# Eleven pad tiles in the SBUF pools of a one-core diffusion block: another start address for the operands of its matmuls

## The chip, the cores and the metric

The kernel runs on one core of one Trainium2 chip. It uses TensorE (PE in the profile, with PEld for its loads of the stationary operand), VectorE (DVE), ScalarE (ACT), GpSimd (POOL) and SyncE (SP), which issues all loads from HBM. The metric is the device time of one execution in microseconds (us); lower is better. SBUF, the core's working memory, has 128 partitions, and a tile lies at the same byte address in each of them. "Phase" below means the start address of an operand in its partition, modulo 256 bytes. "Distance" means the phase of a matmul's moving operand less the phase of its stationary operand, again modulo 256.

## The reference

One block works on 256 latent tokens (`x`) with 256 context tokens (`ctx`), 1024 channels, one layer, all in float32. Cut to what sets the work:

```python
mod = silu(c) @ w_ada + b_ada                       # 9 vectors, for x and for ctx
x   = x   + 0.5 * g1 * swiglu(modulate(rmsnorm(x)),   w13_ffn1, w2_ffn1)   # d_ff 2816
ctx = ctx + 0.5 * g1 * swiglu(modulate(rmsnorm(ctx)), w13_ffn1, w2_ffn1)
q, k, v, g, f, ga, gf = split(modulate(rmsnorm(.)) @ w_in)   # ctx: k and v alone are needed
o   = bidirectional retention, 4 heads (dk 256, dv 512), state from ctx, then x
r   = (silu(g) * groupnorm(o)) @ p_ret
fo  = real(fft2(f over tokens and 256 channels of a group)) @ p_four
x   = x + g2 * ((sigmoid(ga) * r + sigmoid(gf) * fo) @ w_out)
x   = x + 0.5 * g3 * swiglu(modulate(rmsnorm(x)), w13_ffn2, w2_ffn2)
return rmsnorm(x)
```

## The kernel before

Channels lie on partitions and tokens on the free axis. Every float32 product is made of three fp32r matmuls: a weight tile is loaded as `wr`, rounded by ACT into `wh` (line 78), and DVE (sometimes POOL) writes the remainder `wl` (line 79). The activations are split into a high and a low tile in the same way (`split`, lines 82 to 84). `mm3` (lines 86 to 90) then multiplies low weights by high activations, high by low, and high by high into one PSUM bank. The first operand of `mm3` is the stationary one (128 columns); the second is the moving one, with 256, 258 or 512 columns.

PE runs these stages in order. The names are those of the output banks in the profile.

- **`acc`, `pa`, `pb`**: first FFN, up. Moving `h1h`/`h1l` (512 columns: ctx and x side by side). `acc` is the opening, woven with the ada vectors by a hand-written order; `pa` and `pb` follow.
- **`y`**: first FFN, down, in two halves. Moving `gh`/`gl`, 512 columns, and for the last two outputs twice 256.
- **`kc`, `kx`, `q`, `s`, `u`, `o`**: the four heads. Keys of ctx (moving `h2ch`/`h2cl`), keys and queries of x (moving `h2xh`/`h2xl`), scores (moving `qt`, stationary `kt`), sums over tokens (moving `pt`, stationary `ht`) and values (moving `ut`). All have 256 columns.
- **`f`, `sq`, `mx`**: the Fourier branch. In `f` the roles are turned round: the weight tile moves, with 512 columns, and `h2x` is stationary. `sq` moves `dft` over stationary `fu`; `mx` moves `cu` over stationary `dft`.
- **`g`, `gg`, `ro`, `yo`**: gates (moving `h2x`), the two branch projections (moving `gt` and `mx`), the output projection (moving `mg`). 256 columns.
- **`fa`, `fb`**: second FFN, up. Moving `hxh`/`hxl` with 258 columns; two of them carry the shift vector through the product. **`z`**: second FFN, down, moving `g2h`/`g2l`, 256 columns.

Outside the opening, a scheduler sets the order on each engine; the pools set the addresses. A pool is opened on the left or the right side of SBUF (`fpool`, line 50) and its tiles follow each other from that side in the order in which they are made, so that a tile's address is that of its pool plus the sizes of the tiles made before it. Tiles start at multiples of 32 bytes. A 258-column tile of `hx` holds 1032 bytes and so stands 1056 bytes from the next: the phase goes on by 32 from one `hx` tile to the next (`hxh0` 32, `hxl0` 64, `hxh1` 96, and so on). All the other tiles that move or stand have sizes that are multiples of 512 bytes, and keep the phase of their pool. The weight pool `wp` stands at phase 32.

Of the kernel before, what the change touches and what calls it, by code (L numbers as in the profile page):

```python
# [7 lines left out]
F32 = mybir.dt.float32  # L8
F32R = mybir.dt.float32r
BF16 = mybir.dt.bfloat16  # L10
AF = mybir.ActivationFunctionType
ALU = mybir.AluOpType

P = 128
T = 256
D = 1024
KT = D // P
# [9 lines left out]
OUT = (P, KT, T)  # L27
UB = 4
HOOK = 0
TC_KW = dict(schedule_with_timeline_sim=True)  # L30


# [5 lines left out]
def block_kernel(ctx: ExitStack, tc: tile.TileContext, i: dict, out: bass.AP):  # L38
    nc = tc.nc
    V, S, G, PE = nc.vector, nc.scalar, nc.gpsimd, nc.tensor  # L40
# [9 lines left out]
    def fpool(stack, name, side):  # L50
        return stack.enter_context(tc.tile_pool(name=name, bufs=1, reuse_waits="tile", side=side))

    ffn1 = ExitStack()
    hp = fpool(ffn1, "hp", "left")
    gp = fpool(ffn1, "gp", "left")
    ada_stack = ExitStack()
    adp = fpool(ada_stack, "adp", "left")

    def bank(name):
        return psum.tile([P, 512], F32, name=name, tag="ps")  # L60

    def f32(ap):
        return ap.bitcast(F32)

    uid = [0]

    def wtile(t, name):
        return wp.tile([P, 1024], F32 if t == "wr" else F32R, name=name, tag=t, bufs=4)

    def load_w(src, n, lo_engine=None):  # L70

        uid[0] += 1
        raw, hi, lo = [wtile(t, f"{t}{uid[0]}") for t in ("wr", "wh", "wl")]
        dst = raw[:, :n]
        if len(src.shape) == 3:
            dst = dst.rearrange("p (k c) -> p k c", k=src.shape[1])
        nc.sync.dma_start(dst, src)
        S.copy(hi[:, :n], raw[:, :n])  # L78
        (lo_engine or V).tensor_tensor(lo[:, :n], raw[:, :n], f32(hi[:, :n]), op=ALU.subtract)  # L79
        return hi, lo  # L80

    def split(dst_hi, dst_lo, src):
        S.copy(dst_hi, src)
        V.tensor_tensor(dst_lo, src, f32(dst_hi), op=ALU.subtract)
# [60 lines left out]
    for q in range(4):  # L145
        t = per.tile([P, 2, 512], F32, name=f"xs{q}")
# [18 lines left out]
    V.tensor_tensor(ch[1], cr, f32(ch[0]), op=ALU.subtract)  # L165
    S.activation(warm, cr[:, :1], AF.Sqrt, bias=eps, scale=0.0)
    ps = bank("ct")
    for c in range(4):
        PE.transpose(ps[:, c * P : (c + 1) * P], cr[:, c * P : (c + 1) * P], unit_raw)
# [4 lines left out]
    for q in range(4):  # L174
        cb_ps.append(bank(f"cb{q}"))
# [55 lines left out]


    ps_st = bank("st1")
    for k in range(KT):
        if k < T2K:
# [69 lines left out]
    def modulated(dst, st, s, k, rstd, col, name, engine=None, lo=None):  # L305
# [13 lines left out]
        for n, ss in enumerate(s):  # L319
# [7 lines left out]
                op0=ALU.add, op1=ALU.subtract,  # L327
            )

    h = [  # L330
        (hp.tile([P, 512], F32R, name=f"h1h{k}"), hp.tile([P, 512], F32R, name=f"h1l{k}"))
        for k in range(KT)
# [90 lines left out]
    def ffn1_up(m):  # L423
        pa, pb = bank(f"pa{m}"), bank(f"pb{m}")
        if m < M0:
            c = slice(m * 256, (m + 1) * 256)
            srcs = [i["w13a0"][4 * n : 4 * n + 4, :, c].rearrange("k p c -> p k c") for n in range(2)]
        else:
            srcs = [i["w13a"][m - M0, n] for n in range(2)]
        ws = [load_w(src, 1024) for src in srcs]  # L430
        for ab, ps in enumerate((pa, pb)):
            for k in range(KT):
                c = (k % 4) * 256 + ab * P
                mm3(ps, sl(ws[k // 4], slice(None), slice(c, c + P)), h[k], k == 0, k == KT - 1)
        return gated_unit(pa, pb, f"1_{m}")

    def w2_chunks(src, kts):
        ws, k0 = [], 0
        for n in kts:
            w = load_w(src[:, k0 * P : (k0 + n) * P], n * P)  # L440
            ws += [sl(w, slice(None), slice(c * P, (c + 1) * P)) for c in range(n)]
            k0 += n
        return ws
# [112 lines left out]
    def decays(hd):  # L556
# [16 lines left out]
    raw = tp.tile([P, P], F32, name="unit_2", tag="t1k", bufs=2)  # L573
# [6 lines left out]
    mc = fpool(heads, "mc", "right")  # L580
# [2 lines left out]
        for k in range(KT)  # L583
    ]

    ttp = fpool(ctx, "ttp", "left")
    tt = [ttp.tile([P, 512], F32, name=f"tt{n}", tag=f"tt{n}") for n in range(2 * HEADS)]
    ap = fpool(heads, "ap", "right")
    rope = ap.tile([P, 2, T], F32, name="rope")
    nc.sync.dma_start(rope, i["rope"])  # L590
    cos2, sin2 = [rope[:, n, :].unsqueeze(1).to_broadcast([P, 2, T]) for n in range(2)]
    keys, query, sums, probs = [
        [[ap.tile([P, 512], F32R, name=f"{nm}{n}_{x}") for x in range(2)] for n in range(cnt)]
        for nm, cnt in (("kt", 2), ("qt", 1), ("ut", UB), ("pt", 2))
    ]

    ht = [[ap.tile([P, D], F32R, name=f"ht{t}_{x}") for x in range(2)] for t in range(4)]

    def two(a):
        return a.rearrange("p (a t) -> p a t", a=2)  # L600
# [9 lines left out]
    def transposed(s, k, banks):  # L610

        for t in range(2):
            for x in range(2):
                if k % 4 == 0:
                    banks[t, x] = bank(f"ht{s}_{t}_{x}_{k}")
                c = slice((k % 4) * P, (k % 4 + 1) * P)
                PE.transpose(
                    banks[t, x][:, c].bitcast(F32R), (hc2, hx2)[s][k][x][:, t * P : (t + 1) * P], unit
                )
        if k % 4 == 3:  # L620
            c = slice((k // 4) * 512, (k // 4 + 1) * 512)
            for t in range(2):
                S.copy(ht[2 * s + t][0][:, c], banks[t, 0])
                S.copy(ht[2 * s + t][1][:, c], banks[t, 1])

    def first_unit(s, w, a, pss, hook=None):

        banks = {}
        for k in range(KT):
# [3 lines left out]
            transposed(s, k, banks)  # L633
            if hook and k == HOOK:
                hook()
# [42 lines left out]
    def k_weights(hd):  # L678
        return [load_w(i["wk"][hd, n], 1024, None if hd else G) for n in range(2)]
# [78 lines left out]
    fs, fu, cu, mx = {}, [], [], []  # L758

    def fourier_open():  # L760
        heads.close()
        fs["fp"] = fp = fpool(mix, "fp", "right")
        dft = [fp.tile([P, 768], F32R, name=f"dft{n}") for n in range(2)]
        for n in range(2):
            raw = tp.tile([P, 512], F32, name=f"dftr{n}", tag="t2k", bufs=T2K)
            c = slice(n * 384, (n + 1) * 384)
            nc.sync.dma_start(raw[:, :384], i["dft"][:, c])
            split(dft[0][:, c], dft[1][:, c], raw[:, :384])
        fs["dft"] = dft
        for n in range(2):  # L770
            fu.append([[fp.tile([P, 512], F32R, name=f"fu{n}_{e}_{x}") for x in range(2)] for e in range(2)])
        fs["cu"] = [
            [fp.tile([P, 512], F32R, name=f"cu{n}_{x}") for x in range(2)] for n in range(4)
        ]
        mxp = fpool(mix, "mxp", "right")
        for tiles, nm, cnt in ((mx, "mx", 4), (gt, "gt", KT)):
            for n in range(cnt):
                tiles.append([mxp.tile([P, 512], F32R, name=f"{nm}{n}_{x}") for x in range(2)])

    def sum_and_difference(p0, p1, dst, name):  # L780
        a = tp.tile([P, 512], F32, name=f"fa{name}", tag="t2k", bufs=T2K)
# [47 lines left out]
    gt = []  # L829
# [26 lines left out]
    for hd in range(HEADS):  # L856
        last = hd == HEADS - 1
        score_unit(hd)
        if last:
            fourier_open()  # L860
            fourier_in(0)
        else:
            dec[hd + 1] = decays(hd + 1)
            if hd:
                wk = k_weights(hd + 1)
                kx = project(wk, hx2, f"kx{hd + 1}")
            kx_evac(hd + 1, *kx)
        if hd:
            o_norm(hd - 1, sq)
        if not last:  # L870
            kc_evac(*project(wk, hc2, f"kc{hd + 1}"))
        us = u_unit(hd)
        if last:
            fourier_in(1)
        else:
            q_evac(hd + 1, *project(q_weights(hd + 1), hx2, f"q{hd + 1}"))
        sq = o_unit(hd, us)
# [19 lines left out]
    for j in range(KT):  # L897
# [7 lines left out]
        wr = [load_w(i["pret"][j, c], 1024) for c in range(2)]  # L905
# [25 lines left out]
    V.tensor_copy(ap2[:, :, 0:1].rearrange("p k o -> p (k o)"), mod[:, 1, 6 * KT : 7 * KT])  # L931
    W = T + 2
    g2 = fpool(ctx, "g2", "left")
    hx = [
        (g2.tile([P, W], F32R, name=f"hxh{k}"), g2.tile([P, W], F32R, name=f"hxl{k}"))
        for k in range(KT)
    ]
    ssum[0] = per.tile([P, 512], F32, name="ssum3", tag="ssum")
    XC = slice(T, 2 * T)

# [184 lines left out]
```

## Time and profile before

| | us |
|---|---|
| three timed runs, median | 1014.06 (1011.98 to 1014.34) |
| profiled execution | 1015.47 |
| its span, first to last instruction | 1013.7 |
| granted TensorE clock, mean | 0.994 |

Of the span's 1013.7 us, ACT is busy for 469.4 us (46%) and POOL for 62.4 us (6%); 166.84 MB come and go by DMA. The shares are averages over stages with different limits, so a table by stage is needed beside them. Matmuls overlap in their pipeline: each shows a duration longer than the time to the next one's start. What a matmul costs the kernel is the time from its start to the start of the next, called its spacing below. A spacing is read from the timeline: start of the last row less start of the first, over the number of steps between them.

### The profile page before, as it was taken

The page shows a single profiled execution, that of the slowest core. Times are in us where ns is not written, and L with a number is a line of the kernel's source. Part 1 is how long each engine was busy: PE and PEld are TensorE (multiplying, and loading weights), DVE is VectorE, ACT ScalarE, POOL GpSimd, SP SyncE. Part 2 cuts the span into 40 slices and gives each one's busy share as a digit, 9 for nine tenths or more (in the row PEclk, how much of TensorE's full clock was granted, in tenths as well). Part 3 has the DMA queues.
Part 4 walks back from the last instruction along what each step waited for, and adds up shares of the span by engine and source line. Part 5 has one row for each costly group of instructions (what it writes and reads, how often), then busy time and mean ns, then how long its engine had stood idle before and what let it go on. Part 6 is the DMA issues. An engine that isn't in the chain of part 4 may idle for free.

```text
span 1013.7 us, 16779 instructions
## 1 busy us (share of the span) xinstructions
PE 984.4 (97%) x6792; PEld 907.9 (90%) x6792; DVE 663.9 (65%) x1084; ACT 469.4 (46%) x725; POOL 62.4 (6%) x39
## 2 busy tenths in 40 slices
PE   6999999999999998999999998999999989999996
PEld 4778888888888888999999997999999989999995
DVE  7879999998334335866575538865555766676543
ACT  4454322125222423756575456754444545555541
POOL 0000000000000013000000026000000300000011
PEclk9999999999999999999999999999999999999999
DMA  8647766994322233223133434456566446656651
GB/s 337 231 176 249 235 199 212 349 402 160 104 83 75 84 112 115 64 84 125 43 126 108 158 100 150 125 185 183 181 200 187 153 161 186 185 172 182 185 174 42
DMA packets 49238, 166.84 MB, mean 165 GB/s; under 512 B 5380, under 2 KB 7044, under 8 KB 49160
## 3 DMA queue, kind: packets, MB, share of 16 engines
q1 hardware_dynamic: 49160, 165.77, 50.8%
q8 instruction: 53, 0.87, 0.3%
q14 instruction: 25, 0.20, 0.1%
HBM read 164.70 MB, written 1.05 MB: 164 GB/s over the span
## 4 chain that ended last, share of the span: by engine, by line
PE 91%; DVE 4%; ACT 2%; DMA 1%; issue 1%; POOL 0%; DVEq 0%; SPq 0%; ACTq 0%; POOLq 0%
PE y L88 4%; PE y L89 4%; PE y L90 4%; PE pa L89 3%; PE pb L89 3%; PE pa L88 3%; PE pb L88 3%; PE pb L90 3%; PE pa L90 3%; PE ro L89 2%; PE ro L90 2%; PE ro L88 2%; PE fa L89 2%; PE z L90 2%; PE z L89 2%; PE z L88 2%
## 5 line engine op out<-in xcount | busy, mean ns | idle before, releaser
L79 DVE TENSOR_TENSOR wl<-wr,wh 128x1024 fp32r<-128x1024 f32 (+1 forms) x214 | 248.8, 1164 | 202.0 <-ACT wh L78 201.2
L78 ACT CAST wh<-wr 128x1024 fp32r<-128x1024 f32 (+1 forms) x226 | 227.0, 1006 | 273.2 <-PE y L90 79.2
L191 DVE CUSTOM_DVE_ANT_0 junk<-ada,cb,sm 128x1024 bf16<-128x1024 f32 x96 | 122.9, 1280 | 5.9 <-DMA ada<-in_ada 4.4
L89 PE MATMUL y<-gl,wh 128*128 128x512 f32 (+1 forms) x198 | 72.5, 366 | 0.0
L88 PE MATMUL y<-gh,wl 128*128 128x512 f32 (+1 forms) x198 | 72.4, 366 | 0.0
L90 PE MATMUL y<-gh,wh 128*128 128x512 f32 (+1 forms) x198 | 72.3, 365 | 0.0
L455 POOL TENSOR_TENSOR ssum<-ssum,sq 128x256 f32<-128x256 f32 (+1 forms) x18 | 24.6, 1367 | 727.3 <-ACT sq L454 714.2
L89 PE MATMUL pa<-h1l,wh 128*128 128x512 f32 x152 | 59.1, 389 | 0.0
L88 PE MATMUL pa<-h1h,wl 128*128 128x512 f32 x152 | 59.1, 389 | 0.0
L90 PE MATMUL pa<-h1h,wh 128*128 128x512 f32 x152 | 59.1, 389 | 0.0
L88 PE MATMUL pb<-h1h,wl 128*128 128x512 f32 x152 | 59.1, 389 | 0.0
L89 PE MATMUL pb<-h1l,wh 128*128 128x512 f32 x152 | 59.1, 389 | 0.0
L90 PE MATMUL pb<-h1h,wh 128*128 128x512 f32 x152 | 59.1, 389 | 0.0
L89 PE MATMUL fa<-hxl,wh 128*128 128x258 f32 x176 | 50.8, 289 | 0.0
L88 PE MATMUL fa<-hxh,wl 128*128 128x258 f32 x176 | 50.8, 289 | 0.0
L90 PE MATMUL fa<-hxh,wh 128*128 128x258 f32 x176 | 50.6, 287 | 0.0
L89 PE MATMUL fb<-hxl,wh 128*128 128x258 f32 x176 | 50.1, 284 | 0.0
L89 PE MATMUL z<-g2l,wh 128*128 128x256 f32 x176 | 50.0, 284 | 0.0
L88 PE MATMUL fb<-hxh,wl 128*128 128x258 f32 x176 | 50.0, 284 | 0.0
L90 PE MATMUL fb<-hxh,wh 128*128 128x258 f32 x176 | 49.9, 283 | 0.0
L88 PE MATMUL z<-g2h,wl 128*128 128x256 f32 x176 | 49.8, 283 | 0.0
L90 PE MATMUL z<-g2h,wh 128*128 128x256 f32 x176 | 49.8, 283 | 0.0
(310 smaller groups left out, 2908.3 us busy)
## 6 DMA issues: line engine op xcount, KB each, us to landing
ada<-in_ada SPq DMA_DIRECT2D x72, 512.0 KB, 5.1
wr<-in_w13b SPq DMA_DIRECT2D x44, 512.0 KB, 4.3
wr<-in_w13a SPq DMA_DIRECT2D x38, 512.0 KB, 4.3
wrv<-in_wv SPq DMA_DIRECT2D x16, 512.0 KB, 4.3
wr<-in_wg SPq DMA_DIRECT2D x16, 512.0 KB, 4.2
wr<-in_wgate SPq DMA_DIRECT2D x16, 512.0 KB, 4.3
wr<-in_pret SPq DMA_DIRECT2D x16, 512.0 KB, 3.8
wr<-in_w2b SPq DMA_DIRECT2D x16, 512.0 KB, 3.6
```

The source lines that it names most:

```text
L78: S.copy(hi[:, :n], raw[:, :n])
L79: (lo_engine or V).tensor_tensor(lo[:, :n], raw[:, :n], f32(hi[:, :n]), op=ALU.subtract)
L88: PE.matmul(o, w[1], a[0], start=start, stop=False)
L89: PE.matmul(o, w[0], a[1], start=False, stop=False)
L90: PE.matmul(o, w[0], a[0], start=False, stop=stop)
L191: V.tensor_tensor_reduce(junk, raw, cb[:, s, :], 1.0, sm[:, BIAS + n : BIAS + n + 1], ALU.mult, ALU.add, mod[:, s, n : n + 1],)
L455: G.tensor_tensor(ssum[0][:, cols], ssum[0][:, cols], sq[:, :w], op=ALU.add)
```

## The change

A helper `shifted(pool, name, eighths)` makes a tile of `32 * eighths` bytes in a pool and fills it with zeros on DVE. Nothing reads it. It is called at eleven places. The tiles of `hx` become 288 columns long (1152 bytes), and their first 258 columns are used as before. `load_w` now cuts the tiles when it makes them, with an offset `at` that every call leaves at 0. `several` makes the same tiles as the lists that it replaces.

```diff
+LINE = 32
...
+    def shifted(pool, name, eighths):
+
+        if eighths:
+            V.memset(pool.tile([P, 8 * eighths], F32, name=name), 0.0)
...
+    shifted(hp, "pad_hp", 6)
+    shifted(gp, "pad_gp", 7)
     h = [
...
+    shifted(mc, "pad_mc", 1)
     ttp = fpool(ctx, "ttp", "left")
+    shifted(ttp, "pad_ttp", 7)
...
+    keys = several(ap, "kt", 2, 512, 1)
+    query = several(ap, "qt", 1, 512, 0)
+    sums = several(ap, "ut", UB, 512, 0)
+    probs = several(ap, "pt", 2, 512, 5)
+
+    ht = several(ap, "ht", 4, D, 1)
...
+        shifted(fp, "pad_dft", 4)
...
+        fs["cu"] = several(fp, "cu", 4, 512, 5)
...
+    shifted(g2, "pad_g2", 6)
     hx = [
-        (g2.tile([P, W], F32R, name=f"hxh{k}"), g2.tile([P, W], F32R, name=f"hxl{k}"))
+        tuple(g2.tile([P, LINE * -(-W // LINE)], F32R, name=f"{nm}{k}")[:, :W] for nm in ("hxh", "hxl"))
         for k in range(KT)
     ]
+    shifted(g2, "pad_hx", 7)
```

The phases that follow from it, stage by stage (moving, stationary: distance), with the number of fp32r matmuls of each:

| stage | matmuls x columns | before | after |
|---|---|---|---|
| `acc` | 144 x 512 | 32, 32: 0 | 224, 32: 192 |
| `pa`, `pb` | 912 x 512 | 32, 32: 0 | 224, 32: 192 |
| `y` | 462 x 512, 132 x 256 | 32, 32: 0 | 192, 32: 160 |
| `kc` | 192 x 256 | 224, 32: 192 | 192, 32: 160 |
| `kx`, `q` | 384 x 256 | 224, 32: 192 | same |
| `s` | 96 x 256 | 224, 224: 0 | 0, 224: 32 |
| `u` | 384 x 256 | 224, 224: 0 | 0, 160: 96 |
| `o` | 384 x 256 | 224, 32: 192 | 0, 32: 224 |
| `f` | 96 x 512 | 32, 224: 64 | same |
| `sq` | 48 x 256 | 224, 224: 0 | 192, 64: 128 |
| `mx` | 48 x 256 | 224, 224: 0 | 64, 192: 128 |
| `g`, `gg` | 768 x 256 | 224, 32: 192 | same |
| `ro` | 576 x 256 | 224, 32: 192 | 192, 32: 160 |
| `yo` | 192 x 256 | 32, 32: 0 | 0, 32: 224 |
| `fa`, `fb`, moving `hxh` | 704 x 258 | 0, 64, 128, 192 in turn | 192, 32: 160 |
| `fa`, `fb`, moving `hxl` | 352 x 258 | 32, 96, 160, 224 in turn | 64, 32: 32 |
| `z` | 528 x 256 | 32, 32: 0 | 160, 32: 128 |

No instruction changes its place on PE, ACT, POOL or SP. On DVE eleven fills of 8 to 56 columns come in. The first two stand in the opening, between the reciprocal of the first norm and the first product with an ada row. DVE's order there, before:

```order
L257 MEMSET pick 1x128 x4
L228 RECIPROCAL rstd1q<-sd1q 128x128
L191 ISA junk_0_254,mod<-ada_114,cb,sm 128x1024
L191 ISA mod 128x1
L191 ISA junk_1_256,mod<-ada_114,cb,sm 128x1024
```

and with the change:

```order
L263 MEMSET pick 1x128 x4
L234 RECIPROCAL rstd1q<-sd1q 128x128
L63 MEMSET pad_hp 128x48
L63 MEMSET pad_gp 128x56
L197 ISA junk_0_258,mod<-ada_114,cb,sm 128x1024
L197 ISA mod 128x1
L197 ISA junk_1_260,mod<-ada_114,cb,sm 128x1024
```

Here two fills are put in and nothing else moves. Three more stand where the first FFN ends and the heads begin: `xs` is the residual stream that the last `y` bank updates, `h2cl` the low half of the context's modulated input, on which `kc` waits. DVE's order there, before:

```order
L321 SCALAR_TENSOR_TENSOR xr_0_2_3420<-xs_108,amul,rstd_0_3274 128x256
L321 SCALAR_TENSOR_TENSOR xr_0_3_3424<-xs_108,amul,rstd_0_3274 128x256
L460 SCALAR_TENSOR_TENSOR xs_112<-y_7_1_3300,gate,xs_112 128x256
L325 SCALAR_TENSOR_TENSOR h2cl_3343<-xr_0_0_3412,mod,h2ch_3342 128x256
L325 SCALAR_TENSOR_TENSOR h2cl_3345<-xr_0_1_3416,mod,h2ch_3344 128x256
```

and with the change:

```order
L327 SCALAR_TENSOR_TENSOR xr_0_3_3438<-xs_108,amul,rstd_0_3278 128x256
L468 SCALAR_TENSOR_TENSOR xs_112<-y_7_1_3304,gate,xs_112 128x256
L63 MEMSET pad_kt 128x8
L63 MEMSET pad_pt 128x40
L63 MEMSET pad_ht 128x8
L331 SCALAR_TENSOR_TENSOR h2cl_3347<-xr_0_0_3426,mod,h2ch_3346 128x256
L331 SCALAR_TENSOR_TENSOR h2cl_3349<-xr_0_1_3430,mod,h2ch_3348 128x256
```

The three fills stand ahead of the first `h2cl`. The other six stand between operations of DVE in stages in which PE has work queued.

More of the change, by code (lines that the diff above doesn't have):

```diff
@@ L68, in wtile, with load_w @@
         return wp.tile([P, 1024], F32 if t == "wr" else F32R, name=name, tag=t, bufs=4)
-    def load_w(src, n, lo_engine=None):
+    def load_w(src, n, lo_engine=None, at=0):
         uid[0] += 1
-        raw, hi, lo = [wtile(t, f"{t}{uid[0]}") for t in ("wr", "wh", "wl")]
-        dst = raw[:, :n]
+        raw, hi, lo = [wtile(t, f"{t}{uid[0]}")[:, at : at + n] for t in ("wr", "wh", "wl")]
+        dst = raw
         if len(src.shape) == 3:
@@ L77, in load_w @@
         nc.sync.dma_start(dst, src)
-        S.copy(hi[:, :n], raw[:, :n])
-        (lo_engine or V).tensor_tensor(lo[:, :n], raw[:, :n], f32(hi[:, :n]), op=ALU.subtract)
+        S.copy(hi, raw)
+        (lo_engine or V).tensor_tensor(lo, raw, f32(hi), op=ALU.subtract)
         return hi, lo
@@ L591, in block_kernel, with several @@
     cos2, sin2 = [rope[:, n, :].unsqueeze(1).to_broadcast([P, 2, T]) for n in range(2)]
[L592 to L597, printed above, removed]
+    def several(pool, nm, cnt, width, after=0):
+        tiles = [[pool.tile([P, width], F32R, name=f"{nm}{n}_{x}") for x in range(2)] for n in range(cnt)]
+        shifted(pool, f"pad_{nm}", after)
+        return tiles
+    keys = several(ap, "kt", 2, 512, 1)
[3 more added lines that the diff above has]
+    ht = several(ap, "ht", 4, D, 1)
     def two(a):
@@ L771, in fourier_open @@
             fu.append([[fp.tile([P, 512], F32R, name=f"fu{n}_{e}_{x}") for x in range(2)] for e in range(2)])
-        fs["cu"] = [
-            [fp.tile([P, 512], F32R, name=f"cu{n}_{x}") for x in range(2)] for n in range(4)
-        ]
+        fs["cu"] = several(fp, "cu", 4, 512, 5)
         mxp = fpool(mix, "mxp", "right")
-        for tiles, nm, cnt in ((mx, "mx", 4), (gt, "gt", KT)):
-            for n in range(cnt):
-                tiles.append([mxp.tile([P, 512], F32R, name=f"{nm}{n}_{x}") for x in range(2)])
+        mx.extend(several(mxp, "mx", 4, 512, 0))
+        gt.extend(several(mxp, "gt", KT, 512, 0))
     def sum_and_difference(p0, p1, dst, name):
```

## The prediction

> **What bounds the kernel now.** I read the page's busy shares first, then its chain of work that ended last.
>
> ```profile
> PE 984.4 (97%) x6792; PEld 907.9 (90%) x6792; DVE 663.9 (65%) x1084; ACT 469.4 (46%) x725; POOL 62.4 (6%) x39
> ...
> PE 91%; DVE 4%; ACT 2%; DMA 1%; issue 1%; POOL 0%; DVEq 0%; SPq 0%; ACTq 0%; POOLq 0%
> ```
>
> The chain is PE for 91% of the span. A nanosecond on each of the 6792 matmuls is therefore up to 6.8 us of the kernel, if PE is the bound where they stand. Loads of the stationary operand (PEld) are busy for 907.9 us beside PE's 984.4, so nearly every matmul streams its moving operand while the next stationary one is read from the same memory. Next, the table of windows, cut at the stages; after each window come the busy times of PE, PEld and DVE.
>
> ```profile
> 0.00:92.00 92.00, 82.88 (x531) 64.10 (x532) 74.99 (x145) 45.44 (x79) 0.20 (x4) 1.00 0.70 249
> 92.00:158.00 66.00, 66.00 (x293) 54.66 (x292) 62.72 (x96) 19.36 (x25) 0.00 (x0) 1.00 0.68 218
> 158.00:217.00 59.00, 59.00 (x262) 48.87 (x261) 57.26 (x102) 13.86 (x17) 0.00 (x0) 1.00 0.89 320
> ...
> 436.00:561.00 125.00, 125.00 (x1053) 124.79 (x1052) 80.31 (x148) 78.05 (x160) 3.91 (x3) 1.00 0.30 97
> ...
> 670.00:783.00 113.00, 113.00 (x961) 113.00 (x961) 60.93 (x67) 52.49 (x61) 0.00 (x0) 1.00 0.62 188
> ...
> 940.00:1001.00 61.00, 61.00 (x509) 60.95 (x509) 28.36 (x32) 27.12 (x38) 7.46 (x6) 1.00 0.49 143
> ```
>
> Outside the opening (first row) PE is busy in the whole of these windows. DVE has slack in all but two: from 92 to 217 us it is busy for 120.0 of 125 us, so at most 5.0 us can be won there before DVE becomes the bound. The granted clock (third column from the end) is 1.00 throughout, so no difference between stages comes from it. The timeline gives the spacings. Of each pair below, the first and the last row of a stretch in which nothing waits:
>
> ```profile
> 299.77 0.39 PE L88 MATMUL pb<-h1h,wl 128*128 128x512 f32 x1
> ...
> 301.81 0.39 PE L88 MATMUL pb<-h1h,wl 128*128 128x512 f32 x1
> ...
> 561.37 0.40 PE L89 MATMUL f<-wl,h2xh 128*128 128x512 f32 x1
> ...
> 563.47 0.40 PE L89 MATMUL f<-wl,h2xh 128*128 128x512 f32 x1
> ...
> 939.95 0.28 PE L90 MATMUL z<-g2h,wh 128*128 128x256 f32 x1
> ...
> 942.95 0.28 PE L88 MATMUL z<-g2h,wl 128*128 128x256 f32 x1
> ...
> 671.94 0.28 PE L89 MATMUL gg<-h2xl,wh 128*128 128x256 f32 x1
> ...
> 674.88 0.28 PE L90 MATMUL gg<-h2xh,wh 128*128 128x256 f32 x1
> ...
> 481.79 0.28 PE L89 MATMUL kc<-h2cl,wh 128*128 128x256 f32 x1
> ...
> 483.94 0.28 PE L90 MATMUL kc<-h2ch,wh 128*128 128x256 f32 x1
> ```
>
> With 512 columns: `pb`, distance 0, makes 9 steps in 2.04 us, 226.7 ns each; `f`, distance 64, makes 9 in 2.10 us, 233.3 ns. With 256 columns: `z`, distance 0, makes 25 in 3.00 us, 120.0 ns; `gg`, distance 192, makes 25 in 2.94 us, 117.6 ns. So stages of one shape at different distances do differ, by 2 to 7 ns. The last pair warns: `kc` stands at 192 like `gg` and makes 19 steps in 2.15 us, 113.2 ns. **Distance goes with the spacing but does not fix it alone**; for `kc` another state, 4.4 ns shorter, lasts there for a while.
>
> **The change part by part.** What is removed is, at most, a few ns on each matmul of the stages whose distance changes; what is added is eleven fills. For other distances the second FFN helps: its `hx` tiles take all eight in turn, in a fixed weight phase. The bank `fa` begins at 851.75 us, and four cuts of a few ns each show its first four groups of three matmuls (k = 0 to 3), with the mean duration of each row.
>
> ```profile
> 851.63 0.28 PE L90 MATMUL fb<-hxh,wh 128*128 128x258 f32 x1
> 851.75 0.29 PE L88 MATMUL fa<-hxh,wl 128*128 128x258 f32 x1
> ...
> L88 PE MATMUL fa<-hxh,wl 128*128 128x258 f32 x1 | 0.3, 287 | 0.0
> L90 PE MATMUL fa<-hxh,wh 128*128 128x258 f32 x1 | 0.3, 287 | 0.0
> L89 PE MATMUL fa<-hxl,wh 128*128 128x258 f32 x1 | 0.3, 285 | 0.0
> ...
> L89 PE MATMUL fa<-hxl,wh 128*128 128x258 f32 x1 | 0.3, 283 | 0.0
> L90 PE MATMUL fa<-hxh,wh 128*128 128x258 f32 x1 | 0.3, 283 | 0.0
> L88 PE MATMUL fa<-hxh,wl 128*128 128x258 f32 x1 | 0.3, 282 | 0.0
> ...
> L89 PE MATMUL fa<-hxl,wh 128*128 128x258 f32 x1 | 0.3, 286 | 0.0
> L88 PE MATMUL fa<-hxh,wl 128*128 128x258 f32 x1 | 0.3, 284 | 0.0
> L90 PE MATMUL fa<-hxh,wh 128*128 128x258 f32 x1 | 0.3, 282 | 0.0
> ...
> L89 PE MATMUL fa<-hxl,wh 128*128 128x258 f32 x1 | 0.3, 284 | 0.0
> L88 PE MATMUL fa<-hxh,wl 128*128 128x258 f32 x1 | 0.3, 283 | 0.0
> L90 PE MATMUL fa<-hxh,wh 128*128 128x258 f32 x1 | 0.3, 282 | 0.0
> ```
>
> `hxh` stands at distances 0, 64, 128, 192 and `hxl` at 32, 96, 160, 224. By distance the durations are: 0: 287; 32: 285; 64: 282.5; 96: 283; 128: 283; 160: 286; 192: 282.5; 224: 284 ns. Zero is the worst, 160 nearly as bad, the others 2 to 4.5 ns shorter. I take the difference from 287 as the difference in spacing from distance 0, for 256 columns also. It is an assumption, since here each distance follows another one.
>
> - 256 columns, from distance 0 (spacing 120.0): `s` 96 x -2 = -0.19 us; `u` 384 x -4 = -1.54; `sq` and `mx` 96 x -4 = -0.38; `yo` 192 x -3 = -0.58; `z` 528 x -4 = -2.11; the short `y` 132 x -1 = -0.13. Sum -4.93. Bounds: no gain, since 120.0 is the longest steady spacing of this shape, and 113.2, which is 6.8 ns on 1428, or -9.7.
> - 256 columns, from distance 192 (117.6): `kc` and `ro` go to 160, where 120.0 - 1 = 119.0, so 768 x +1.4 = +1.08 us; `o` goes to 224, 120.0 - 3 = 117.0, so 384 x -0.6 = -0.23. Bounds for the 1152: 113.2 (-5.1) and 120.0 (+2.8).
> - 258 columns: the twelve durations have a mean of 284.0. With the change, every group of three is 160, 32, 160: (286 + 285 + 286) / 3 = 285.7. So 1056 x +1.67 = +1.76 us. Bounds: all at 282 (-2.1) and at 287 (+3.2).
> - 512 columns: `pa` and `pb` go from 0 to 192. The nearest row with these two distances in one shape is `z` against `gg`, -2.4 ns; 912 of these give -2.19 us. `y` goes to 160: 462 x -1 = -0.46. Bounds: up to `f`'s 233.3, +6.7 on 1374, or +9.2 us; down by the same step, -9.2. `acc` (144) counts for nothing: PE waits in the opening, 82.88 of 92 us busy, and a shorter matmul there meets the same wait. If that cover is gone it is 144 x -2.4 = -0.35.
> - The fills. Two fills of DVE from the groups by shape, DVE's row in the opening, and the wait of PE at the start of the heads:
>
> ```profile
> L118 DVE MEMSET ones<- 128x128 f32 x1 | 0.2, 165 | 0.0
> ...
> L531 DVE MEMSET ls<- 128x8 f32 x1 | 0.1, 65 | 0.0
> ...
> 14.47 1.28 DVE L191 CUSTOM_DVE_ANT_0 junk<-ada,cb,sm 128x1024 bf16<-128x1024 f32 x1 [0.56 <-DMA sm<-in_smalls]
> ...
> PE ht L617 <- ACT h2ch L324: 1.9, 1, 1.9
> ```
>
> A fill of 8 columns takes 65 ns and one of 128 takes 165; those of 32 to 56 lie between, 100 as an estimate on the line through the two. The first two (0.2 us) stand where DVE waits 0.56 us for a DMA, which hides them; without it they would cost 0.2. `kt`, `pt` and `ht` (65 + 100 + 65 = 230 ns) stand ahead of the `h2cl` products, for which `kc` and its transposes queue on PE, which already waits there for this normalisation. I count them in full: +0.2 us. Their tiles were freed by earlier stages, and the fills bring no wait of their own: the scheduled order gives none of the eleven one. The other six, some 0.5 us in all, lie beside PE stages with slack on DVE. Were that slack gone, all eleven would cost 0.9.
>
> **The sum.** -4.93 + 1.08 - 0.23 + 1.76 - 2.19 - 0.46 + 0.2 = -4.8 us, of the profiled execution's 1015.47, which gives 1010.7. That execution was 1.4 us above the median of the timed runs; against that median of 1014.06 it is **1009.3 us**.
>
> A rule that speaks against the change: the Trainium skill, "TensorE: Matmul & The Clock Gate", section "Step-by-step: what each phase is for", says that PE reads the moving and the stationary operand through two independent ports, and that loading the next weights takes no read bandwidth from the running matmul. By that rule the distance would be worth nothing and the time would be 1014.3. The 120.0 of `z` against the 117.6 of `gg` speaks against it here, though it does not prove that distance is the cause.
>
> The same page's section "Back-to-back issue gap" gives N / 2.4 + 2.5 ns for a warm matmul alone. As an estimate that is 215.8 ns for 512 columns, against the 226.7 of `pb`; by it the 512-column term would be 1374 x -10.9 = -15.0 us. No stretch of this trace shows that spacing.
>
> **The rivals.**
>
> *A: the 512-column stages get longer.* `f` is the only long stretch with 512 columns away from distance 0, and it is longer, not shorter, by 6.7 ns. If any distance but 0 brings that step, `pa`, `pb` and `y` give +9.2 us in place of -2.65, and the time is 1014.06 - 2.12 + 9.2 = 1021.1 us. The kernel is slower as soon as these 1374 matmuls lose more than 2.12 / 1374 = 1.5 ns each. Against it: `f` has its roles turned round, and with 258 columns distance 64 is among the best.
>
> *B: the new distances free most of the collisions.* The 113.2 ns of `kc` show what a 256-column matmul can do here. If the changed stages settle there, the terms reach their lower bounds: -9.7 - 5.1 - 9.2 - 2.1 + 0.2 = -25.9, and 988.2 us. For it: that state holds for the 19 steps shown, and distance 0, which never shows it in `z`'s stretch, is the commonest before. Against it: `gg` at the same distance 192 does not stay in it. DVE permits it: the 512-column share between 92 and 217 us is 125 / 0.2267 = 551 matmuls x 6.7 = 3.7 of its 5.0 us.
>
> *C: the change does not do what it says.* If the differences between stages come from what else runs beside them, only the fills are left: 1014.3 us.
>
> **How the numbers follow.** My forecast with its own range of 1003 to 1013 has a chance of 0.42, B or at least half of it 0.20, C 0.17, A or most of it 0.21. The range runs from 996 to 1021: the forecast, C, about half of A and half of B lie in it, and some 0.18 outside. A measurement of this kernel tells about 0.3%, 3 us, from no change, so faster is below 1011.0 and slower above 1017.1. Faster: 0.32 of the forecast, all of B, 0.01 of C, 0.53. Slower: 0.16 of A and 0.01 of C, 0.17. The rest is 0.30.
>
> **What would show it.** In the changed profile: `z` and `u` near 116 ns spacing where I expect -4; near 113 speaks for B, at 120 for C. `pa` and `pb` near 224; 233 speaks for A. `ro` a little longer than 117.6, about 119. `fa` and `fb` longer by under 2 ns. `g`, `gg`, `kx`, `q` and `f`, whose distances stay, should keep 117.6 and 233.3; if they move too, something else than distance is at work. I would be wrong most easily in carrying durations of mixed distances at 258 columns to steady stretches of 256 and 512.

## The result and the profile after

The change made the kernel **slower by 0.6%**: 1020.71 us (median of six runs, 1016.32 to 1021.07) against 1013.44 (six runs beside them, 1011.98 to 1014.74), a ratio of 1.0063 with a 95% interval of 1.005 to 1.0076. In microseconds that is +6.4, from 5.1 to 7.7. The profiled execution of the change took 1016.32 us with a span of 1014.5; it was the fastest of its six, so the two profiled executions differ by 0.85 us only, far less than the medians. The page of the changed kernel, busy shares and chain:

```profile
PE 985.9 (97%) x6792; PEld 899.6 (89%) x6792; DVE 665.0 (66%) x1095; ACT 468.9 (46%) x725; POOL 62.3 (6%) x39
...
PE 91%; DVE 4%; ACT 2%; issue 1%; DMA 1%; POOL 0%; DVEq 0%; SPq 0%; ACTq 0%; POOLq 0%
```

Nothing here tells where the time went: PE is the bound as before, and DVE has its eleven fills more. The windows do (columns as before: window, its length, busy PE, PEld, DVE, ACT and POOL with their instructions, granted clock, DMA share, GB/s):

```profile
0.00:92.00 92.00, 83.25 (x538) 63.36 (x539) 76.89 (x150) 46.21 (x80) 0.20 (x4) 1.00 0.73 252
92.00:158.00 66.00, 66.00 (x285) 53.17 (x284) 60.72 (x93) 18.27 (x24) 0.00 (x0) 1.00 0.70 215
158.00:217.00 59.00, 59.00 (x253) 47.43 (x252) 55.91 (x98) 13.36 (x17) 0.00 (x0) 1.00 0.88 309
...
670.00:783.00 113.00, 113.00 (x969) 113.00 (x969) 62.28 (x69) 54.42 (x63) 0.00 (x0) 1.00 0.63 188
806.00:940.00 134.00, 130.85 (x1089) 130.60 (x1088) 95.97 (x190) 70.77 (x99) 7.57 (x4) 1.00 0.59 180
940.00:1001.00 61.00, 61.00 (x514) 60.95 (x513) 29.35 (x33) 28.07 (x39) 7.46 (x6) 1.00 0.51 149
```

PE is just as full, but what it gets done has changed, and in both directions. Where `pa`, `pb` and `y` run with 512 columns (second and third row) 285 matmuls fit where 293 did, and 253 where 262 did; DVE is less busy there (60.72 us after 62.72), so the loss isn't DVE's. In the 256- and 258-column stages (last rows) slightly more fit: 969 after 961, 514 after 509.

The timeline of the changed kernel gives the spacings. Of each pair below, the first and last row of a stretch without a wait:

```profile
179.99 0.39 PE L95 MATMUL y<-gl,wh 128*128 128x512 f32 x1
...
181.86 0.40 PE L94 MATMUL y<-gh,wl 128*128 128x512 f32 x1
...
299.85 0.39 PE L95 MATMUL pa<-h1l,wh 128*128 128x512 f32 x1
...
301.95 0.39 PE L95 MATMUL pa<-h1l,wh 128*128 128x512 f32 x1
...
452.43 0.28 PE L96 MATMUL u<-pt,ht 128*128 128x256 f32 x1
...
455.43 0.28 PE L95 MATMUL u<-pt,ht 128*128 128x256 f32 x1
...
675.84 0.28 PE L94 MATMUL gg<-h2xh,wl 128*128 128x256 f32 x1
...
678.90 0.28 PE L94 MATMUL gg<-h2xh,wl 128*128 128x256 f32 x1
...
689.40 0.28 PE L94 MATMUL gg<-h2xh,wl 128*128 128x256 f32 x1
...
692.47 0.28 PE L96 MATMUL gg<-h2xh,wh 128*128 128x256 f32 x1
...
945.86 0.28 PE L94 MATMUL z<-g2h,wl 128*128 128x256 f32 x1
...
948.95 0.28 PE L96 MATMUL z<-g2h,wh 128*128 128x256 f32 x1
```

- `y` makes 8 steps in 1.87 us, 233.8 ns; `pa` 9 in 2.10, 233.3. Before, `pb` beside `pa` took 226.7.
- `u` makes 25 steps in 3.00 us, 120.0 ns: at distance 96 it is no shorter than `z` was at 0. `z`, now at 128, makes 26 in 3.09 us, 118.8: shorter by 1.2.
- `gg`, whose distance didn't change, has two spacings: 27 steps in 3.06 us, 113.3 ns, and 14 us later 26 in 3.07, 118.1.

Summed start to start over each whole stage, changed kernel less the one before, in the two profiled executions:

| stages | us |
|---|---|
| `pa`, `pb`, `y` (512 columns) | +3.02, +3.04, +3.51: **+9.57** |
| `s`, `u`, `o` | -0.30, 0.00, +0.60 |
| `sq`, `mx`, `kc`, `ro`, `yo`, `z` | +0.14, -0.05, +0.23, +0.14, -0.31, -0.68 |
| `fa`, `fb` | -2.32, -0.62 |
| `f`, `kx`, `q`, `gg` (distance not changed) | -0.22, -0.32, -0.58, -0.82 |
| `g` (distance not changed, has waits in it) | -1.58 |
| the opening (`acc`, transposes, sums, waits), the short `y` | -1.8, -0.22 |

So +9.57 us in 1374 matmuls, and some -8.7 in all the rest, of which part belongs to these two executions and not to the change (experiment 4).

### The profile page after: what moved, and what is told of

Its sections match the earlier page's. It is cut to its first block, busy times and chain, and to the rows that moved or that the text cites. A ratio compares the mean times of both kernels' runs of the same rounds, so it can differ in the third digit from the quotient of the medians.

```text
span 1014.5 us, 16790 instructions
## 1 busy us (share of the span) xinstructions
PE 985.9 (97%) x6792; PEld 899.6 (89%) x6792; DVE 665.0 (66%) x1095; ACT 468.9 (46%) x725; POOL 62.3 (6%) x39
## 4 chain that ended last, share of the span: by engine, by line
PE 91%; DVE 4%; ACT 2%; issue 1%; DMA 1%; POOL 0%; DVEq 0%; SPq 0%; ACTq 0%; POOLq 0%
PE y L94 4%; PE y L96 4%; PE y L95 4%; PE pa L94 3%; PE pb L94 3%; PE pb L95 3%; PE pa L95 3%; PE pa L96 3%; PE pb L96 3%; PE ro L96 2%; PE ro L95 2%; PE ro L94 2%; PE z L95 2%; PE z L94 2%; PE z L96 2%; PE fb L95 2%
```

## The experiments

All are made from the changed kernel or the one before by the widths of the pads, in units of 32 bytes; no order of instructions is touched.

### 1 and 2: the two pads of the first FFN, taken out and put in alone

The theory is that the 512-column stages lose about 9.5 us by their distance and the rest wins about 5. Experiment 1 undoes the pads of `hp` and `gp` in the changed kernel:

```diff
-    shifted(hp, "pad_hp", 6)
-    shifted(gp, "pad_gp", 7)
```

> The changed kernel without pad_hp and pad_gp: the 512-column stages pa, pb and y go back to distance 0, all other distances stay changed. Theory (the 512-column matmuls lose a step of 6.7 ns or more at the new distances, and that is all that makes the change slower): pa, pb and y at 226.7 ns, the trace some 9.6 us shorter there, about 1009 to 1012 us, faster than before or the same. Rival 1 (the loss is in other stages or in the fills, or comes and goes with the execution): the time stays near 1018 to 1021 us. Rival 2 (the 256-column stages win nothing, and the 512-column ones are the whole difference): 1013 to 1014 us.

Measured: 1009.96 us (ten runs, 1006.85 to 1012.44) against 1013.52 of before, a ratio of 0.9963 (0.9949 to 0.9977). Experiment 2 is the kernel before with these two pads and no other:

```diff
+    shifted(hp, "pad_hp", 6)
+    shifted(gp, "pad_gp", 7)
```

> The kernel before with pad_hp and pad_gp alone. Theory: pa and pb at 233.3 and y at about 234 ns, so +9.6 us, 1022 to 1024 us, and every stage behind them as before: 117.8 for gg and ro, 120.0 for z and u. Rival 1 (the loss is elsewhere): no change from before, 1013 us. Rival 2 (the rest of the change wins nothing): 1020 to 1021 us, as the whole change.

Measured: 1024.77 us (four runs, 1022.2 to 1025.78), a ratio of 1.0102 (1.0081 to 1.0123), just above the 1022 to 1024 expected. The timelines of both in the up product, first of experiment 1:

```profile
299.90 0.39 PE L96 MATMUL pb<-h1h,wh 128*128 128x512 f32 x1
...
301.94 0.39 PE L96 MATMUL pa<-h1h,wh 128*128 128x512 f32 x1
```

and of experiment 2:

```profile
299.96 0.39 PE L96 MATMUL pb<-h1h,wh 128*128 128x512 f32 x1
...
301.83 0.39 PE L95 MATMUL pa<-h1l,wh 128*128 128x512 f32 x1
```

Experiment 1 makes 9 steps in 2.04 us, 226.7 ns as before; experiment 2 makes 8 in 1.87, 233.8. By whole stages experiment 1 has `pa`, `pb` and `y` at 0.00 against before, and its other steady stages as in the changed kernel (`q` -0.58, `gg` -0.82, `z` -0.68); experiment 2 has +3.02, +3.05 and +3.51, and `gg`, `ro`, `u`, `z`, `yo` and `f` at 0.00. **The change is two parts that add up**: two pads that cost 9.6 us by the stages (10.3, from 8.2 to 12.5, by experiment 2's times), and nine with the longer `hx` tiles that win 3.7 us (2.3 to 5.2). Together that is +6.6 us, where the whole change measured +6.4.

### 3 and 4: is a spacing chance?

`gg` moved although its distance stayed, and the changed kernel's six times spread by 4.8 us. I thought that an execution might fall into one set of spacings or another; the rival was that the addresses fix the spacings and that the spread comes from elsewhere. Experiment 3 is the changed source with all pads zero and the old tile length, thus the addresses of before; experiment 4 is the changed kernel again.

```diff
-    shifted(hp, "pad_hp", 6)
+    shifted(hp, "pad_hp", 0)
...
-LINE = 32
+LINE = 2
```

> All pads at 0: the addresses and the order of the kernel before, profiled once more. Question: is the spacing of a stage fixed by its distance, or does it differ from one execution to the next? If fixed: every stage within 0.1 ns of the first profile, gg and ro at 117.8. If it depends on how a stage is entered, and that is the same each time: the same, kc of heads 1 and 2 at 113.3 again. If it is chance: gg or g in places at 113.3 where they had 117.8, and the sum of the 192-distance stages off by 1 us or more.

> The changed kernel profiled once more. Its first profile was its fastest timed execution, 1016.3 us beside a median of 1020.7. Theory: in the first profile q, g and half of gg stood at 113.3 ns, which the slower executions do not do; so here, at 1018 to 1021 us, these stages show 117.8, with pa and pb at 233.3 as before. Rival: the stages show the same spacings, and the 4 us are in waits or in throttled clock windows.

Measured: 1014.54 us and 1019.59 us, one run each. These stages of experiment 3 equal those of before to 0.01 us (`gg` 45.23, `ro` 67.84, `z` 64.77, `u` 46.24). Those of experiment 4 equal the first profile of the changed kernel (`pa` +3.01, `q` -0.58, `gg` -0.82, `z` -0.69), though its time is 3.3 us longer. So for these stages my theory fell and the rival held. One stage does not repeat: `fb`, with 258 columns, is 0.26 us shorter in experiment 3 than before, at the same addresses. Both timelines over the same 192 steps of `fa` and `fb`, with no wait in them and a granted clock of 1.00, first of before:

```profile
851.75 0.29 PE L88 MATMUL fa<-hxh,wl 128*128 128x258 f32 x1
...
875.11 0.29 PE L88 MATMUL fa<-hxh,wl 128*128 128x258 f32 x1
```

and of experiment 3:

```profile
851.23 0.28 PE L94 MATMUL fa<-hxh,wl 128*128 128x258 f32 x1
...
874.48 0.28 PE L94 MATMUL fa<-hxh,wl 128*128 128x258 f32 x1
```

That is 121.7 ns a step and 121.1. Here a spacing does differ from one execution to the next. Where the 3.3 us of experiment 4 are is seen in its windows:

```profile
0.00:92.00 92.00, 82.96 (x533) 63.74 (x534) 75.55 (x149) 45.24 (x79) 0.20 (x4) 0.94 0.72 250
...
806.00:940.00 134.00, 130.84 (x1077) 130.47 (x1077) 95.51 (x191) 70.14 (x97) 8.14 (x5) 0.99 0.59 179
```

The granted clock is 0.94 in the opening and 0.99 from 806 to 940 us, where the first profile shows 1.00 twice; 533 matmuls fit into the first window instead of 538, and 1077 into the other instead of 1089. The kernel before has 0.99 there as well:

```profile
806.00:940.00 134.00, 131.04 (x1064) 130.78 (x1063) 91.69 (x186) 69.68 (x96) 4.87 (x2) 0.99 0.57 175
```

So about 1.1 us of `fa`'s -2.32 (it is -1.19 in experiment 4) belong to an execution, not to the change; another 0.7 us of the 3.3 are waits of `kc` and the transposes beside it. The opening's -1.8 belong to an execution as well. The row of before shows a clock of 1.00 there, but its profile has no record of the clock ahead of 25.9 us, and its matmuls were slow. First before, then the changed kernel:

```profile
22.51 0.63 PE L89 MATMUL acc<-h1l,wh 128*128 128x512 f32 x1
...
24.22 0.63 PE L90 MATMUL acc<-h1h,wh 128*128 128x512 f32 x1
```

```profile
21.47 0.39 PE L96 MATMUL acc<-h1h,wh 128*128 128x512 f32 x1
...
22.17 0.40 PE L96 MATMUL acc<-h1h,wh 128*128 128x512 f32 x1
```

Before makes 4 steps in 1.71 us, 427 ns each, as experiment 4 does at its low clock; the changed kernel makes 3 in 0.70, 233.

`g` is -1.58 here, but +1.65 in experiment 3, whose addresses are those of before, so its waits differ by as much between executions. Not all of the -1.58 is waits: the 380 steps of `g` without one took 44.37 us before, 43.42 with the change and 43.40 in experiment 4, so 0.95 us are a shorter spacing. Without the parts that belong to an execution the table comes to +0.9 + 1.1 + 1.8 + 0.6 = about +4.4, somewhat below the interval of the times; where the rest lies these traces do not show. The six times themselves go with the clock: the two executions of the changed kernel with a mean granted clock of 0.995 took 1016.32 and 1018.03 us, the four with 0.991 or 0.992 took 1020.51 to 1021.07.

### 5: distance or phase?

In experiment 2 the phase of `h1` and its distance to the weights changed together. Here the weights move too, by 64 bytes, so that `h1` keeps distance 192 and has its old phase of 32 again, while `gh` has distance 0 at the new phase 96. All the other pads are zero and `hx` has its old length; the 256-column stages that were at 192 stand at 128, `f` at 128, `yo` and `z` at 0 with 96 over 96.

```diff
+    shifted(wp, "pad_wp", 2)
...
     shifted(hp, "pad_hp", 6)
-    shifted(gp, "pad_gp", 7)
+    shifted(gp, "pad_gp", 2)
```

> The kernel before with the weight pool moved by 64 bytes and h1 moved back, so that h1 moves at phase 32 as before, over weights at phase 96 (distance 192), and gh at phase 96 over 96 (distance 0). Theory (the distance of the two operands sets the spacing, not the phase of one): pa and pb at 233.3 though h1 is where it was, y at 226.7 though gh is not; yo and z (96 over 96) at 120.0. Rival (the phase of the moving operand alone): pa and pb at 226.7, y at something else. Rival 2 (the phase of the stationary one): pa, pb and y alike.

Measured: 1019.73 us. From its timeline:

```profile
180.05 0.39 PE L96 MATMUL y<-gl,wh 128*128 128x512 f32 x1
...
181.86 0.39 PE L95 MATMUL y<-gh,wl 128*128 128x512 f32 x1
...
300.04 0.39 PE L96 MATMUL pa<-h1l,wh 128*128 128x512 f32 x1
...
301.90 0.39 PE L95 MATMUL pb<-h1h,wl 128*128 128x512 f32 x1
```

`y` at 0 makes 8 steps in 1.81 us, 226.3 ns, though both its operands have moved; `pa` at 192 makes 8 in 1.86, 232.5, though its moving operand stands at the phase of before. By whole stages `pa` is +3.02 and `y` +0.06. `yo` and `z` at 0 take 120.0 again. **The distance decides, not the phase.**

### 6, 7 and 9: the other distances

Three kernels scan the distances, from the kernel before, with four pads each (`hp`, `gp`, `ttp` for the output projection, `hx` for `z`): 1, 1, 1, 1; then 3, 1, 2, 3; then 7, 7, 3, 4.

```diff
+    shifted(hp, "pad_hp", 1)
+    shifted(gp, "pad_gp", 1)
...
+    shifted(ttp, "pad_ttp", 1)
...
+    shifted(g2, "pad_hx", 1)
```

> The kernel before with h1 at distance 32, gh at 64, mg at 32, g2h at 64. What is the spacing at the other distances? Theory (512 columns: any distance but 0 costs a step): pa and pb at 233 or more, y at 233.3, as f has at 64. Rival (only some distances are bad): one of them at 226.7 or at 220. With 256 columns, from the durations of the second FFN before: yo at 32 about 118, z at 64 about 115.5; from the runs so far (s at 32: 117, z at 128: 119) rather 117 to 119.

> The same with h1 at distance 96, gh at 128, mg at 64, g2h at 160. Theory: pa, pb and y at 233 or more. Rival: one of them at 226.7 or below. 256 columns: yo at 64 between 115.5 and 119, z at 160 between 118 and 120, as ro and kc in the changed kernel.

> The kernel before with h1 at distance 224, gh at 192, mg at 96, g2h at 224: the last distances. 512 columns so far: 0 gives 226.7; 32, 96, 128, 192 give 233.3; 160 gives 234.3; 64 gives 228.9 in y and 227 to 233 in f. Theory (0 is the shortest for 512 columns): pa and pb at 224 above 226.7, 228 to 234; y at 192 at 233.3 as pa was, so that the stage does not matter. Rival: 224 below 226.7. 256 columns: yo at 96 117 to 120, z at 224 117 to 119.

Measured: 1016.34, 1024.79 and 1021.39 us, one run each. One distance with 512 columns stands between the two levels, `y` at 64 in experiment 6:

```profile
179.97 0.39 PE L94 MATMUL y<-gh,wl 128*128 128x512 f32 x1
...
181.80 0.39 PE L96 MATMUL y<-gh,wh 128*128 128x512 f32 x1
```

8 steps in 1.83 us, 228.8 ns. With 256 columns the short `y` of the same run, also at 64, has a spacing that the other stages at 64 don't show:

```profile
388.29 0.28 PE L94 MATMUL y<-gh,wl 128*128 128x256 f32 x1
...
394.98 0.28 PE L96 MATMUL y<-gh,wh 128*128 128x256 f32 x1
```

59 steps in 6.69 us are 113.4 ns; behind a wait, from 400.63 us on, the same stage takes 117.6 (17 steps in 2.00 us). Steady spacings by distance, from all the runs so far:

| distance | 512 columns, ns | 256 columns, ns |
|---|---|---|
| 0 | 226.7 | 120.0 |
| 32 | 233.3 | 116.7 |
| 64 | 228.9 (`y`), 228.8 to 233.5 (`f`) | 113.3 (short `y`) or 117.8 |
| 96 | 233.3 | 120.0 |
| 128 | 233.3 (`y`), 232.7 (`f`) | 118.7 |
| 160 | 234.3 | 117.2 to 119.0 |
| 192 | 233.3 | 113.3 or 117.8 |
| 224 | 233.3 | 118.0 to 118.4 |

**The two shapes want opposite things.** For 512 columns 0 is the best distance, for 256 it is, with 96, the worst. For 256 columns 192 and 64 alone show anything below 116.7, and both show two values; at 64 the short one stands in one stage only.

### 8: each shape at its best distance

If the table holds, a kernel with the 512-column stages at 0 and all stages of 256 and 258 columns at 192 should beat both. Its edits against the changed kernel (the short `y` stays at 0, `f` at 64):

```diff
-LINE = 32
+LINE = 64
...
-    shifted(hp, "pad_hp", 6)
-    shifted(gp, "pad_gp", 7)
...
-    shifted(mc, "pad_mc", 1)
-    shifted(ttp, "pad_ttp", 7)
+    shifted(ttp, "pad_ttp", 6)
...
-    keys = several(ap, "kt", 2, 512, 1)
-    query = several(ap, "qt", 1, 512, 0)
+    keys = several(ap, "kt", 2, 512, 6)
+    query = several(ap, "qt", 1, 512, 2)
...
-    probs = several(ap, "pt", 2, 512, 5)
-    ht = several(ap, "ht", 4, D, 1)
+    probs = several(ap, "pt", 2, 512, 2)
+    ht = several(ap, "ht", 4, D, 6)
...
-        shifted(fp, "pad_dft", 4)
+        shifted(fp, "pad_dft", 2)
+        shifted(fp, "pad_fu", 4)
-        fs["cu"] = several(fp, "cu", 4, 512, 5)
+        fs["cu"] = several(fp, "cu", 4, 512, 2)
...
-    shifted(g2, "pad_g2", 6)
...
-    shifted(g2, "pad_hx", 7)
```

> A kernel that puts each stage where the runs so far show its shortest spacing: 512 columns (acc, pa, pb, y) at distance 0, every 256- and 258-column stage at 192 (hx tiles of 1280 bytes, so that all of them stand at 192). Theory 1 (a stage at 192 takes 113.3 or 117.8 according to how it is entered, and comes into 117.8 from stages at distance 0): with no stage at 0 among them, the heads and gates keep 113.3 for most of the way, about 2600 x 4.4 + 1300 x 6.7 ns, 15 to 20 us, 994 to 1000 us. Theory 2 (117.8 is the usual state at 192 and 113.3 the exception): z, u, s and yo win 2.2 ns, 3 us, and the second FFN some 2 us: 1007 to 1010 us.

Measured: **1000.46 us** (five runs, 998.34 to 1001.26) against 1014.26, a ratio of 0.9860 (0.9841 to 0.9878). From its windows and its timeline:

```profile
670.00:783.00 113.00, 113.00 (x1000) 113.00 (x999) 62.10 (x73) 52.66 (x61) 0.00 (x0) 1.00 0.61 191
```

```profile
671.90 0.28 PE L96 MATMUL ro<-gt,wh 128*128 128x256 f32 x1
...
674.96 0.28 PE L96 MATMUL ro<-gt,wh 128*128 128x256 f32 x1
...
934.85 0.28 PE L95 MATMUL z<-g2l,wh 128*128 128x256 f32 x1
...
937.91 0.28 PE L95 MATMUL z<-g2l,wh 128*128 128x256 f32 x1
```

1000 matmuls fit where before has 961; `ro` and `z` make 27 steps in 3.06 us each, 113.3 ns. By whole stages against before: `z` -3.47, `ro` -2.56, `u` -2.08, `gg` -1.71, `yo` -1.16, -11.0 of the -14.2 us between the two profiled executions. Theory 1 expected 994 to 1000 us and theory 2 1007 to 1010, so the time lies just above the range of theory 1. `ro` and `gg` stand at 192 in both kernels and yet moved. `fa` and `fb` didn't win much: -0.77 and +0.31.

### 10: what decides between the two spacings at 192?

The stages `g`, `gg`, `ro` and `yo` stand behind and among `sq` and `mx`, 96 matmuls that were at 0 before. This kernel is experiment 8 with only these two back at 0:

```diff
-        shifted(fp, "pad_dft", 2)
-        shifted(fp, "pad_fu", 4)
-        fs["cu"] = several(fp, "cu", 4, 512, 2)
+        fs["cu"] = several(fp, "cu", 4, 512, 0)
```

> The kernel of the run before (e8_best) with one thing undone: sq and mx, 96 matmuls of 256 columns, back at distance 0. Theory (a stage at 192 keeps the state in which it is entered, and a stage at 0 hands on the longer one): g after the last mx, gg, ro and yo go from 113.3 to 117.8 although their distances stay at 192: about 1270 x 4.4 ns = 5 to 6 us for 96 matmuls moved, 1005 to 1007 us. Rival (each stage's spacing is set by its own distance alone, and the rest of e8_best's gain has another cause): gg and ro stay at 113.3, the loss is under 0.7 us, 1000 to 1001 us.

Measured: 1004.60 us (four runs, 1003.74 to 1006.89), a ratio of 0.9915 (0.9894 to 0.9937). From its windows and its timeline:

```profile
670.00:783.00 113.00, 113.00 (x962) 113.00 (x961) 59.36 (x65) 49.87 (x58) 0.00 (x0) 1.00 0.61 187
```

```profile
671.85 0.28 PE L94 MATMUL ro<-gt,wl 128*128 128x256 f32 x1
...
674.91 0.28 PE L96 MATMUL ro<-gt,wh 128*128 128x256 f32 x1
```

26 steps in 3.06 us, 117.7 ns, and 962 matmuls where experiment 8 had 1000: `gg` (45.23 us) and `ro` (67.84) are those of before again, though nothing of theirs differs from experiment 8. `sq` and `mx` themselves take 0.17 us more. The trace of before shows the same step inside one stage, `g` ahead of the first `sq` and behind the second:

```profile
606.87 0.28 PE L88 MATMUL g<-h2xh,wl 128*128 128x256 f32 x1
...
609.82 0.28 PE L90 MATMUL g<-h2xh,wh 128*128 128x256 f32 x1
...
616.86 0.28 PE L90 MATMUL g<-h2xh,wh 128*128 128x256 f32 x1
...
619.81 0.28 PE L88 MATMUL g<-h2xh,wl 128*128 128x256 f32 x1
```

26 steps take 2.95 us, 113.5 ns, and behind `sq` 25 steps take 2.95, 118.0. In the traces of before and of this kernel, from 560 to 680 us, every stretch at 192 that follows one at 0 without a wait between is at the longer spacing, and it keeps it to its end: the last `mx` is at 120, and the last 138 matmuls of `g`, then `gg` and `ro` (here `yo` too, which stands at 0 in before) stay near 118. In experiment 8 the last `g` is at 113 and all four stay near it. In all seven traces with `sq` and `mx` at 0 and `gg` at 192, `gg` takes 45.2 us; in the two with all three at 192 (experiments 8 and 11) it takes 43.52. **What stands ahead of `gg` and `ro` decides between their two spacings.**

It isn't a matter of distance 0 alone: in experiment 8, where all stand at 192, the `o` that ends at 512 us is at 113 and the `s` behind it at 118. Nor do the addresses settle it everywhere: the last `o`, behind `f`, has the same distances in experiments 8 and 10, and runs at 118 in the one and at 113 in the other. And `z`, behind the second FFN, is at 113 in both kernels.

### 11: another distance for the second FFN

`fa` and `fb` at 192 (experiment 8) took 120.8 ns in steady stretches; in the changed kernel, at 160 and 32 in turn, 120.0. So experiment 8 with these two, while `z` stays at 192:

```diff
-LINE = 64
+LINE = 32
...
+    shifted(g2, "pad_g2", 7)
...
+    shifted(g2, "pad_hx", 1)
```

> The kernel e8_best with hx at distances 160 and 32 in turn, as in the changed kernel, and the rest at 192 as it was. Theory: fa and fb at 120.3 in place of 121.1 ns, -0.8 us; z enters from another state, 113.3 as before or 117.8, which would cost 2.3 us. So 999.5 or 1002 us. Rival (the pads on hx do nothing by themselves): 1000.5, fa and fb at 121.

Measured: **999.75 us** (four runs, 999.18 to 1000.15), a ratio of 0.9864 (0.9849 to 0.9879). `fa` and `fb` together are 1.23 us shorter than in experiment 8, at 120.0 ns again, `yo` is 0.40 longer and `z` stays at 113.3; the two kernels can't be told apart by their ratios. Both beat the kernel before by 1.4%.

## Why the prediction was wrong

The forecast was 1009.3 us, faster; the result is slower, and close to rival A. By the steps:

- **The step that failed is the 512-column term.** The prediction sized it by `z` against `gg`, 256-column stages, and got -2.19 for `pa` and `pb` and -0.46 for `y`. They measured +6.06 and +3.51: 12.2 us of error in one term. The row for it was there: `f`, with 512 columns and away from 0, at 233.3 against 226.7. It was put down as a bound with the argument that its roles are turned round, and a row of another shape was carried instead. Rival A, which went by `f`, gave +9.2; measured +9.57. Experiments 1, 2 and 5 show that these pads, and the distance that they make, are the cause.
- **256 columns from distance 0.** Predicted -4.93, measured about -1.4. `s` -0.19 against -0.30; `yo` -0.58 against -0.31; the short `y` -0.13 against -0.22; `sq` and `mx` -0.38 against +0.09: small and near. `u` failed, -1.54 against 0.00, and `z`, -2.11 against -0.68: 258-column durations in which each distance follows another one said 4 ns for 96 and 128, and steady stretches show 0 and 1.2. The warning on this step was right, and should have been a wider price.
- **256 columns from 192.** `kc` and `ro` +1.08 predicted, +0.37 measured; `o` -0.23 predicted, +0.60 measured. Within their bounds.
- **258 columns.** +1.76 predicted, about -1.8 measured (experiment 4's `fa` -1.19 and `fb` -0.62): below zero instead of above, from the same carried durations. Against experiment 3, whose addresses are those of before, it is -1.1, so part of the size belongs to an execution.
- **The fills and `acc`** cost next to nothing that can be seen. With openings that ran alike, `acc` is +0.09 (experiment 4 against before) and +0.10 (the first profile against experiment 3): in the opening PE waits for others, as the step said. The prediction's reading of a clock of 1.00 in the first window was wrong, as `acc` at 427 ns shows (experiment 4); no term of its sum rests on it.
- **The unchanged stages.** The prediction said that if `q`, `g`, `gg` and `f` moved, something else than distance would be at work. They moved, by -0.2 to -1.6 us (part of the latter waits), and something else is: experiment 10 shows for `gg` and `ro` that it is the stage ahead; for `kx`, `q` and `f` that is argued, not shown. Rival B's second spacing is real. The prediction knew it from `kc` alone; the rows of `g` in experiment 10 were in the trace of before as well, and would have told that `sq` at 0 stands between the two.
- **Rivals.** C fell with experiment 2: two pads alone made 1374 matmuls 6.6 to 7.6 ns longer. With it fell what the prediction drew from the rule of the two independent ports (the Trainium skill, "TensorE: Matmul & The Clock Gate", section "Step-by-step: what each phase is for"), that distance is worth nothing. B came true only in experiments 8 and 11, with other distances, and to about half of its 25.9 us. A named the right mechanism and the right size for these stages; that its total of 1021.1 falls on the median is partly luck, since its other terms were not right either.

By the Trainium skill, "TensorE: Matmul & The Clock Gate", section "Back-to-back issue gap", a warm matmul alone with 256 columns would take an estimated 109.2 ns (256 / 2.4 + 2.5). The shortest steady stretch in any run here is 113.3.

What stays open: why 512 columns want distance 0 and 256 columns do not; what the two spacings at 192 and 64 are inside PE, and what else than the stage ahead selects between them; and what made `fa` and `fb` differ between two executions of the same addresses. That operands meet in the memory where they are read is an inference from the part that distance plays, not shown.

## What to carry to other kernels

When an effect is carried from one stage to another, take the row of the same shape first, even if something else about it differs: here the effect changes its sign between 256 and 512 columns. In this kernel, where PE is the bound, the relative address of the two operands was worth anything from +1.0% (experiment 2) to -1.4% (experiments 8 and 11), and it's best tried stage by stage (four pads, four stages, one run), reading the spacing in the timeline rather than the total time, which varies by several us between executions. A stage that moves although nothing of its own was changed points to the stage ahead of it, or to the execution: a second profile of the same kernel tells the two apart.

## What the runs showed of the hardware

- fp32r matmuls of one shape have several steady spacings, which go with the distance of the operands within 256 bytes: 226.7 to 234.3 ns with 512 columns, 113.3 to 120.0 with 256. In another execution of the same addresses they repeated to 0.03 us per stage (experiment 3, the stages `pa`, `pb`, `y`, `q`, `s`, `u`, `gg`, `ro`, `yo`, `z`); the exception is `fb`, with 258 columns, -0.26 us.
- At distance 192 with 256 columns there are two, 113.3 and 117.8 ns, and what stands ahead can select: moving 96 matmuls back to distance 0 cost 4.1 us (1004.60 against 1000.46; the ratios to before are 0.9915 and 0.9860), of which 0.17 us in these matmuls themselves.
- The granted clock can be low in the opening of an execution: 0.83 in the first 30 us of experiment 4, against 1.00 in the first profile of the same kernel. The rows of that window, of experiment 4 and of the first profile:

```profile
0.00:30.00 30.00, 21.62 (x168) 15.57 (x168) 21.95 (x52) 15.29 (x28) 0.20 (x4) 0.83 0.85 319
```

```profile
0.00:30.00 30.00, 21.90 (x187) 15.43 (x188) 22.95 (x54) 15.78 (x30) 0.20 (x4) 1.00 0.88 332
```

168 matmuls fit into the 30 us of the one, 187 into those of the other. A clock of 1.00 in such a row is no proof: before shows 1.00 there too, with 163 matmuls and `acc` at 427 ns.
